# Both halves of x under one weight load, and a rearranged first stage, in a two-layer encoder on one core

## The chip, the cores and the metric

One core of one Trainium2 chip runs the whole program in one launch. The metric is device time in microseconds (us) per execution; lower is better. The profile is one further execution of the same program, recorded by the hardware profiler. TensorE is called PE, its weight loads PEld, VectorE DVE, ScalarE ACT, GpSimd POOL; SP only issues DMAs here.

## The reference

A sequence of 256 tokens of width 2048 is normalised and sent through two layers. Each layer projects it by one wide matrix, runs four attentions on the pieces, gates and sums their projections, and normalises again:

```
x = layer_norm(x, emb_ln_g, emb_ln_b)
for l in range(2):
    h = x @ w_in[l]                     # 2048 columns -> q, k, v, z of A, B, C, D and the gates
    ya, yb, yc, yd = attentions(h)      # A and D rotate part of q and k, B has a bias, C normalises q and k
    proj = (y * silu(z)) @ w_branch[l]  # for each of the four
    merged = sum(proj * sigmoid(gates + b_gate[l]))
    x = layer_norm(ALPHA * x + merged @ w_out[l], ln_g[l], ln_b[l])
```

All is float32.

## The kernel before

**Three products for one.** Matmuls run on a rounded float32 type. To keep float32 accuracy, x and each weight are split in a high part (the rounded value) and a low part (the rest). A product is then high·high + low·high + high·low. For x the parts are the tiles `th` and `tl` (each 128 x 16 x 256: 16 tiles of 128 features, 256 tokens). For a weight they are `whi`, made by a cast on ACT (line 140), and `wlo`, made by a subtraction on DVE (line 141). Weights come in groups of 512 KB (`wraw`, four buffers, loaded by SP), and each group is split into one of four buffers of `whi` and `wlo`.

**Two ways to project.** `chunk` (lines 172 to 198) puts tokens on the partitions of the result: x's tile is the stationary operand, 512 (or 384) weight columns move, three matmuls for each k and each half of the tokens (lines 182, 183, 186). `chunk_t` (lines 200 to 216) makes transposed columns for the q and k of A, B and D: 128 weight columns are the stationary operand, 256 tokens move. For each k of 16 and each of four blocks of 128 columns it issues three matmuls into the same half bank:

```
nc.tensor.matmul(o, lhsT=hi[:, kk, cs], rhs=tl[:, k, :], ...)   # line 212
nc.tensor.matmul(o, lhsT=hi[:, kk, cs], rhs=th[:, k, :], ...)   # line 213
nc.tensor.matmul(o, lhsT=lo[:, kk, cs], rhs=th[:, k, :], ...)   # line 214
```

A layer has ten such calls (A and B two each, D six), the program twenty. The accumulators are PSUM banks from the pool `psw` (four); a call of either function takes two. A and D then rotate the result (`rotate`, lines 307 to 314), and A and B split it for their score matmuls (`split_evac`, lines 218 to 225, `qkT`).

**First stage.** `first_chunk` (lines 551 to 594) overlaps the first normalisation with the first 512 columns of the projection. Half 0 of x (tokens 0 to 127) is centred on DVE (line 535), transposed on PE in four parts `c` (`x_t`, line 542), scaled on ACT (line 545), and multiplied unsplit with the raw weights (line 571, "plain" below). Half 1 goes the same way, but is split, and multiplied in the three-product form (lines 587, 588, 591, "split pass"). The split of half 0 is made for later columns. `keep_x` (lines 596 to 610) finishes x's scale and shift row-wise and stores it to DRAM; the generator is stepped through in the first stage's neighbours.

**What sets the order.** The code is traced in program order, and a scheduler then orders the instructions of each engine; pools decide what waits for a buffer. Inside `manual_schedule` (line 670) the instructions of PE, ACT and DVE keep the written order among themselves, while others may be put between them. Attention is written as generators (`attend_a` and so on) that advance one step at each weight group (`step`).

Of the kernel before, what the change touches and what calls it, by code (L numbers as in the profile page):

```python
# [88 lines left out]
def hybrid_encoder(ctx: ExitStack, tc: tile.TileContext, a: dict, out: bass.AP):  # L89
# [28 lines left out]
    th = big.tile([P, NK, SEQ], F32R, name="th")  # L118
    tl = big.tile([P, NK, SEQ], F32R, name="tl")
# [4 lines left out]


    def load_raw(src, off, n):
        raw = wrw.tile([P, KG, NCH], F32, tag="wraw", name="wraw")
        nc.sync.dma_start(
            out=raw[:, :, :n],
            in_=src[off:off + P * KG * n].rearrange("(p k n) -> p k n", p=P, k=KG),  # L130
        )
        return raw

    def split_w(raw, n, spare=None, eng=None):
        if spare is None:
            hi = whl.tile([P, KG, NCH], F32R, tag="whi", name="whi")
            lo = whl.tile([P, KG, NCH], F32R, tag="wlo", name="wlo")
        else:
            hi, lo = ((ysp if tag == "yl" else att).tile([P, KG, NCH], F32R, tag=tag, name="wsp", bufs=bufs) for tag, bufs in spare)
        nc.scalar.copy(hi[:, :, :n], raw[:, :, :n])  # L140
        (eng or nc.vector).tensor_tensor(out=lo[:, :, :n], in0=raw[:, :, :n], in1=hi[:, :, :n].bitcast(F32), op=ALU.subtract)  # L141
        return hi, lo

    def load_w(src, off, n, spare=None):
        return split_w(load_raw(src, off, n), n, spare)
# [26 lines left out]
    def chunk(src, off, n, nkt, lh, ll, perm=False, apart=False):  # L172

        acc = [psw.tile([P, NCH], F32, tag="pw", name="pw") for _ in range(2)]
# [23 lines left out]
        return [t[:, :n] for t in acc]  # L198

    def chunk_t(src, off):  # L200

        acc = [psw.tile([P, NCH], F32, tag="pw", name="pw") for _ in range(2)]
        ng = NK // KG
        for g in range(ng):
            hi, lo = load_w(src, off + g * P * KG * NCH, NCH)
            for b in range(4):
                o = acc[b // 2][:, (b % 2) * SEQ:(b % 2 + 1) * SEQ]
                cs = slice(b * P, (b + 1) * P)
                for kk in range(KG):
# [97 lines left out]
    def rotate(ps, dst, rows, cos, sin):  # L307

        xs = att.tile([P, 1024], F32, tag="rb", name="xs", bufs=1)[:rows, :NCH].rearrange("p (n j m) -> p n j m", n=2, j=2)
        for r in range(0, rows, 32):  # L310
            nc.scalar.copy(xs[r:r + 32], ps[r ^ 32:(r ^ 32) + 32])  # L311
        nc.vector.tensor_tensor(out=dst, in0=ps[:rows], in1=cos, op=ALU.mult)
        nc.vector.tensor_tensor(out=xs, in0=xs, in1=sin, op=ALU.mult)
        nc.vector.tensor_tensor(out=dst, in0=dst, in1=xs, op=ALU.add)
# [200 lines left out]
    nc.scalar.dma_start(out=gT, in_=a["emb_ln_gT"])  # L515
    nc.scalar.dma_start(out=bT, in_=a["emb_ln_bT"])

    def load_x(half):
        for c in range(4):
            nc.sync.dma_start(out=merged[:, half, c * NCH:(c + 1) * NCH], in_=a["x"][half * P:(half + 1) * P, c * NCH:(c + 1) * NCH])  # L520

    def center(half):

# [9 lines left out]
        for c in range(4):  # L533
# [17 lines left out]
    def first_chunk(src, off):  # L551
# [16 lines left out]
        for c in range(4):  # L568
# [3 lines left out]
            if c == 0:  # L572
                center(1)
# [344 lines left out]
```

## Time and profile before

| | |
|---|---|
| median of 3 runs | 2149.33 us (2148.49 to 2150.35) |
| the profiled execution's own time | 2148.79 us |
| its span, first to last instruction | 2147.0 us |
| PE busy | 2115.2 us, 99% of the span |
| DVE busy | 1292.0 us, 60% |
| ACT busy | 984.4 us, 46% |
| moved by DMA | 410.55 MB, mean 191 GB/s |
| mean granted PE clock | 0.997 |

Busy time of PE is modelled at the ends of matmuls, so it tells that PE hardly rests, not that every matmul runs at its peak. The distance from one start to the next tells what a matmul costs in a row. The clock that the throttle granted is shown as a share of full speed (2.4 GHz); 0.5 is 1.2 GHz. It is recorded from its first change on, so in the first 16 us the rows' durations have to tell it.

### The profile page before, as it was taken

Reading aid. Unit: us, or ns where it says so; the run is one execution under the profiler, and the core shown is the slowest. Engines: PE = TensorE matmul, PEld = TensorE weight load, DVE = VectorE, ACT = ScalarE, POOL = GpSimd, SP = SyncE. Lnnn points to the kernel's source line nnn. Section 1 sums busy time; section 2 is a strip of 40 time slices with the busy share of each in tenths; the row PEclk is TensorE's granted clock in tenths of the full one; section 3 lists DMA queues with packets and bytes.
Section 4 is the critical chain, followed back from the end, with each engine's and each line's share of the span. In section 5 each row is a group of like instructions: output and inputs, shape, how many; then the busy total and the mean of one; then the engine's idle time right before and its main releaser. Section 6 shows DMA issues by size and latency. Waiting matters only on the chain.

```text
span 2147.0 us, 29625 instructions
## 1 busy us (share of the span) xinstructions
PE 2115.2 (99%) x11720; PEld 1852.4 (86%) x11720; DVE 1292.0 (60%) x1555; ACT 984.4 (46%) x1279; POOL 32.7 (2%) x34
## 2 busy tenths in 40 slices
PE   6999999999999999999999999999999999999997
PEld 4899888888999988888888998888889999888886
DVE  6765655765555565556576655557655555555566
ACT  5554444444454444444445544444444454444442
POOL 0000100000000000000000000000000000000000
PEclk9999999999999999999999999999999999999999
DMA  8755566555555566666755555665555555566664
GB/s 252 232 171 167 190 200 199 186 184 192 186 166 175 166 198 204 215 196 220 229 199 173 168 168 186 199 194 183 185 202 177 176 157 186 193 203 211 198 213 150
DMA packets 129659, 410.55 MB, mean 191 GB/s; under 512 B 13872, under 2 KB 31280, under 8 KB 129008
## 3 DMA queue, kind: packets, MB, share of 16 engines
q1 hardware_dynamic: 129232, 408.64, 59.3%
q8 instruction: 92, 1.51, 0.3%
q14 instruction: 47, 0.39, 0.1%
q10 hardware_dynamic: 288, 0.02, 0.0%
HBM read 402.31 MB, written 6.29 MB: 190 GB/s over the span
## 4 chain that ended last, share of the span: by engine, by line
PE 95%; DMA 2%; DVE 2%; ACT 1%; issue 1%; SPq 0%; DVEq 0%; POOL 0%; ACTq 0%
PE pw L182 23%; PE pw L183 23%; PE pw L186 23%; PE pw L212 7%; PE pw L214 7%; PE pw L213 7%; PE pw L571 1%; PE pt L277 1%; DMA lnr<-in_emb_ln_b 1%; PE po L503 1%; PE po L431 1%; PE sc L489 1%; PE sc L363 0%; DMA lnr<-in_emb_ln_g 0%; PE pt L741 0%
## 5 line engine op out<-in xcount | busy, mean ns | idle before, releaser
L141 DVE TENSOR_TENSOR wlo<-wraw,whi 128x1024 fp32r<-128x1024 f32 (+1 forms) x720 | 864.2, 1203 | 702.6 <-ACT whi L140 702.1
L140 ACT CAST whi<-wraw 128x1024 fp32r<-128x1024 f32 (+1 forms) x720 | 742.7, 1033 | 984.8 <-PE pw L183 681.6
L182 PE MATMUL pw<-whi,tl 128*128 128x512 f32 (+1 forms) x1968 | 760.4, 386 | 0.4 <-DVE tl L222 0.4
L183 PE MATMUL pw<-whi,th 128*128 128x512 f32 (+1 forms) x1968 | 753.6, 383 | 0.0
L186 PE MATMUL pw<-wlo,th 128*128 128x512 f32 (+1 forms) x1968 | 593.4, 383 | 0.0
L182 PEld LDWEIGHTS pw<-whi,tl 128*128 128x128 f32 x1968 | 371.6, 189 | 65.3 <-DVE tl L222 0.6
L183 PEld LDWEIGHTS pw<-whi,th 128*128 128x128 f32 x1968 | 371.7, 189 | 64.7
L186 PEld LDWEIGHTS pw<-wlo,th 128*128 128x128 f32 x1968 | 368.7, 189 | 67.9
L212 PE MATMUL pw<-tl,whi 128*128 128x256 f32 x1280 | 366.9, 287 | 0.0
L214 PE MATMUL pw<-th,wlo 128*128 128x256 f32 x1280 | 362.1, 283 | 0.0
L213 PE MATMUL pw<-th,whi 128*128 128x256 f32 x1280 | 362.1, 283 | 0.0
L212 PEld LDWEIGHTS pw<-tl,whi 128*128 128x128 f32 x1280 | 245.3, 192 | 1.0
L213 PEld LDWEIGHTS pw<-th,whi 128*128 128x128 f32 x1280 | 245.4, 192 | 0.4
L214 PEld LDWEIGHTS pw<-th,wlo 128*128 128x128 f32 x1280 | 245.2, 192 | 0.0
L182 PE MATMUL pw<-whi,yl 128*128 128x512 f32 x256 | 100.7, 393 | 0.0
L183 PE MATMUL pw<-whi,yh 128*128 128x512 f32 x256 | 99.7, 390 | 0.0
L186 PE MATMUL pw<-wlo,yh 128*128 128x512 f32 x256 | 79.4, 390 | 0.0
L186 PEld LDWEIGHTS pw<-wlo,yh 128*128 128x128 f32 x256 | 48.1, 188 | 10.1
L183 PEld LDWEIGHTS pw<-whi,yh 128*128 128x128 f32 x256 | 48.1, 188 | 9.5
L182 PEld LDWEIGHTS pw<-whi,yl 128*128 128x128 f32 x256 | 48.1, 188 | 9.5
L311 ACT COPY xs<-pw 32x512 f32<-32x512 f32 x80 | 46.2, 577 | 11.3 <-PE pw L214 8.3
L759 DVE TENSOR_TENSOR gt<-pw,bg 128x512 f32<-128x512 f32 x64 | 43.9, 687 | 9.2 <-PE pw L186 9.2
(150 smaller groups left out, 1101.2 us busy)
## 6 DMA issues: line engine op xcount, KB each, us to landing
wraw<-in_w_in SPq DMA_DIRECT2D x544, 512.0 KB, 3.6
wraw<-in_w_branch SPq DMA_DIRECT2D x64, 512.0 KB, 3.4
wraw<-in_w_out SPq DMA_DIRECT2D x64, 512.0 KB, 4.2
wraw<-in_w_in SPq DMA_DIRECT2D x64, 384.0 KB, 3.5
bg<-in_b_gate SPq DMA_DIRECT2D x32, 256.0 KB, 4.3
xr<-x_dram SPq DMA_DIRECT2D x16, 256.0 KB, 4.5
merged<-in_x SPq DMA_DIRECT2D x8, 256.0 KB, 5.8
x_dram<-merged SPq DMA_DIRECT2D x8, 256.0 KB, 3.9
```

The lines of the kernel that those rows point to most:

```text
L140: nc.scalar.copy(hi[:, :, :n], raw[:, :, :n])
L141: (eng or nc.vector).tensor_tensor(out=lo[:, :, :n], in0=raw[:, :, :n], in1=hi[:, :, :n].bitcast(F32), op=ALU.subtract)
L182: nc.tensor.matmul(acc[half][:, :n], lhsT=tok(ll, k, half, perm), rhs=hi[:, kk, :n], start=k == 0, stop=False)
L183: nc.tensor.matmul(acc[half][:, :n], lhsT=tok(lh, k, half, perm), rhs=hi[:, kk, :n], start=False, stop=False)
L186: nc.tensor.matmul(acc[half][:, :n], lhsT=tok(lh, k, half, perm), rhs=lo[:, kk, :n], start=False, stop=k == nkt - 1)
L212: nc.tensor.matmul(o, lhsT=hi[:, kk, cs], rhs=tl[:, k, :], start=k == 0 and b % 2 == 0, stop=False)
L213: nc.tensor.matmul(o, lhsT=hi[:, kk, cs], rhs=th[:, k, :], start=False, stop=False)
L214: nc.tensor.matmul(o, lhsT=lo[:, kk, cs], rhs=th[:, k, :], start=False, stop=k == NK - 1 and b % 2 == 1)
L277: nc.tensor.transpose(pt[:, q * P:(q + 1) * P], src[:, q * P:(q + 1) * P], ident)
L311: nc.scalar.copy(xs[r:r + 32], ps[r ^ 32:(r ^ 32) + 32])
L431: nc.tensor.matmul(po[:, hh * P:(hh + 1) * P], lhsT=pT[:, (2 * hh + kt) * P:(2 * hh + kt + 1) * P], rhs=v[:, kt, vcol[hh]:vcol[hh] + P], s ...
L759: nc.vector.tensor_tensor(out=t, in0=ps[half], in1=bg, op=ALU.add)
```

## The change

Four things change.

- **x's parts side by side.** `th` and `tl` become the two halves of one tile `tx` (128 x 16 x 2 x 256). In `chunk_t` one matmul with 512 moving columns takes the place of lines 212 and 213: the stationary high weight meets low and high x at once and writes a full bank, low product in the left half, high product in the right. The low weight's matmul (256 columns) adds to the right half. A weight group is now four k by 256 columns instead of two k by 512, so each call makes 256 columns, in two banks, and there are forty calls.
- **A fold behind it.** The two halves of each bank have to be added: ACT copies the left half to SBUF, DVE adds the right half (`fold`). `rotate` then works on that SBUF tile in place; for D, ACT's copy of the 64 rows that aren't rotated falls away.
- **First stage.** 40 transposes of the identity matrix, whose result nothing reads, stand ahead of all else on PE. The written order is new: parts 0 and 1 of half 0 are transposed ahead of the first plain group, each later part one group ahead; half 1 is centred after the third plain group.
- **Loads.** The first x pieces are issued from SP and ACT in turn; SP is scheduled by hand too; the small weights (`small_weights`) and the rows of `keep_x` are issued behind the last weight load written so far, and `keep_x` is stepped through after A's two attentions.

```
+    tx = big.tile([P, NK, 2, SEQ], F32R, name="tx")
+    tl, th = tx[:, :, 0], tx[:, :, 1]
...
+        for g in range(NK // TG):
+            hi, lo = load_w(src, off + g * P * TG * TCH, TCH, kg=TG)
+            for b in range(2):
                 cs = slice(b * P, (b + 1) * P)
...
+                for kk in range(TG):
+                    k = g * TG + kk
+                    nc.tensor.matmul(acc[b], lhsT=hi[:, kk, cs], rhs=tx[:, k].rearrange("p h t -> p (h t)"), start=k == 0, stop=False)
+                    nc.tensor.matmul(acc[b][:, SEQ:], lhsT=lo[:, kk, cs], rhs=th[:, k, :], start=False, stop=k == NK - 1)
             step()
...
+    def fold(acc, dst, order=None):
+
+        t = vec.tile([P, 2, SEQ], F32, tag="tmp", bufs=3, name="fo")
+        for b in range(2):
+            nc.scalar.copy(t[:, b], acc[b][:, :SEQ])
+            x, y = acc[b][:, SEQ:], t[:, b]
+            if order:
+                x, y = order(x), order(y)
+            nc.vector.tensor_tensor(out=dst[:, b], in0=x, in1=y, op=ALU.add)
...
+            eng = nc.sync if c % 2 == 0 else nc.scalar
+            eng.dma_start(out=merged[:, half, c * NCH:(c + 1) * NCH], in_=a["x"][half * P:(half + 1) * P, c * NCH:(c + 1) * NCH])
...
+        idle = psa.tile([P, NCH], F32, tag="pa", name="idle")
+        for _ in range(WARM):
+            nc.tensor.transpose(idle[:, :P], ident, ident)
```

**PE, start of the program, before.** `pt` is a transposed piece of x, `xt` its scaled copy; lines 571 are the plain matmuls of half 0.

```order
L542 MATMUL pt<-ident,merged 128x128 x4
L571 MATMUL pw<-wraw,xt 128x512 x4
L542 MATMUL pt<-ident,merged 128x128 x4
L571 MATMUL pw<-wraw,xt 128x512 x4
L542 MATMUL pt<-ident,merged 128x128 x4
L571 MATMUL pw<-wraw,xt 128x512 x4
L542 MATMUL pt<-ident,merged 128x128 x8
L571 MATMUL pw<-wraw,xt 128x512 x4
L542 MATMUL pt<-ident,merged 128x128 x4
L587 MATMUL pw<-whi,tl 128x512
```

**PE, start of the program, now.** Line 617 is the warm-up, 558 the transposes, 595 the plain matmuls, 602 the split pass.

```order
L617 MATMUL idle<-ident 128x128 x40
L558 MATMUL pt<-ident,merged 128x128 x8
L595 MATMUL pw<-wraw,xt 128x512 x4
L558 MATMUL pt<-ident,merged 128x128 x4
L595 MATMUL pw<-wraw,xt 128x512 x4
L558 MATMUL pt<-ident,merged 128x128 x4
L595 MATMUL pw<-wraw,xt 128x512 x4
L558 MATMUL pt<-ident,merged 128x128 x4
L595 MATMUL pw<-wraw,xt 128x512 x4
L558 MATMUL pt<-ident,merged 128x128 x4
L602 MATMUL pw<-whi,tx 128x512
```

Each plain group now stands one group of transposes behind the one that it needs, where before it stood right behind it. Further on, the order before puts 56 matmuls of the first `chunk_t` (28 and 28) between the parts of the split pass; now all of the split pass stands ahead of the first `chunk_t`.

**ACT, first stage, now** (line 145 casts weights, 561 scales transposed x, 235 casts x's high part; `xt` with a number is half 1). The first cast stands ahead of all scaling, and two casts of the next weights, the `whi` rows, stand between the last two parts of half 1.

```order
L145 CAST whi<-wraw 128x1024
L561 ACTIVATE xt<-pt,bT,gT 128x128 x8
L145 CAST whi<-wraw 128x1024
...
L235 CAST tx<-xt_299 128x4x128
L145 CAST wsp<-wraw 128x1024 x2
L561 ACTIVATE xt_331<-pt,bT,gT 128x128 x4
L688 ACTIVATE le<-ls 128x2
L145 CAST whi<-wraw 128x1024
L235 CAST tx<-xt_331 128x4x128
L561 ACTIVATE xt_355<-pt,bT,gT 128x128 x4
L145 CAST whi<-wraw 128x1024
L235 CAST tx<-xt_355 128x4x128
```

**ACT, end of the first `chunk_t` call, now** (line 226 is the fold's copy, 325 the rotation's). Before, the rotation's four copies stood there alone, reading PSUM. The first copy now waits for PE's last matmul into the first bank, and casts are queued behind it.

```order
L145 CAST whi<-wraw 128x1024 x3
L226 COPY fo<-pw 128x256
L145 CAST whi<-wraw 128x1024
L226 COPY fo<-pw 128x256
L325 COPY xs<-xr 32x512 x4
L145 CAST whi<-wraw 128x1024 x2
L235 CAST qkT<-xr 128x512
```

## Rows read from the trace of the kernel before

**Rows 1.** The page: PE's busy time, and the chain that ended last, by engine.

```profile
PE 2115.2 (99%) x11720; PEld 1852.4 (86%) x11720; DVE 1292.0 (60%) x1555; ACT 984.4 (46%) x1279; POOL 32.7 (2%) x34
...
PE 95%; DMA 2%; DVE 2%; ACT 1%; issue 1%; SPq 0%; DVEq 0%; POOL 0%; ACTq 0%
```

**Rows 2.** Stretches: length, busy us (count) of PE, PEld, DVE, ACT, POOL; clock, DMA.

```profile
9.30:60.50 51.20, 42.91 (x168) 28.19 (x169) 36.92 (x53) 30.07 (x56) 2.67 (x4) 0.93 0.86 263
...
100.00:1080.00 980.00, 979.96 (x5441) 863.12 (x5440) 583.59 (x690) 450.14 (x573) 14.72 (x12) 1.00 0.60 191
```

**Rows 3.** Stretches of `chunk_t` alone and `chunk` alone; two starts at 384 columns.

```profile
550.36:596.42 46.06, 46.06 (x385) 46.05 (x384) 23.21 (x25) 20.99 (x25) 0.00 (x0) 1.00 0.56 178
266.64:402.75 136.11, 136.11 (x602) 112.65 (x602) 77.21 (x76) 57.90 (x62) 1.33 (x1) 1.00 0.60 196
...
596.43 0.34 PE L182 MATMUL pw<-whi,tl 128*128 128x384 f32 x1
...
596.60 0.34 PE L183 MATMUL pw<-whi,th 128*128 128x384 f32 x1
```

**Rows 4.** Timeline of PE, first stage: start, length, instructions [idle before, and what ended it].

```profile
9.30 1.12 PE L542 MATMUL pt<-ident,merged 128*128 128x128 f32 x4 [9.30 <-DVE merged L535]
10.96 6.28 PE L571 MATMUL pw<-wraw,xt 128*128 128x512 f32 x8 [0.55 <-ACT xt L545]
17.08 0.60 PE L542 MATMUL pt<-ident,merged 128*128 128x128 f32 x4
18.23 3.70 PE L571 MATMUL pw<-wraw,xt 128*128 128x512 f32 x8 [0.55 <-ACT xt L545]
...
26.46 1.04 PE L542 MATMUL pt<-ident,merged 128*128 128x128 f32 x8
29.66 5.40 PE L571 MATMUL pw<-wraw,xt 128*128 128x512 f32 x8 [2.17 <-ACT xt L545]
...
49.51 0.50 PE L587 MATMUL pw<-wsp,tl 128*128 128x512 f32 x1 [2.82 <-DVE tl L222]
...
60.07 0.61 PE L591 MATMUL pw<-wsp,th 128*128 128x512 f32 x2
```

**Rows 5.** Stretches in which the granted clock (third from the end) is low.

```profile
30.00:32.00 2.00, 2.00 (x3) 0.70 (x3) 0.43 (x2) 2.00 (x4) 1.12 (x3) 0.50 0.88 281
50.00:52.00 2.00, 2.00 (x8) 1.54 (x7) 2.00 (x3) 0.00 (x0) 0.00 (x0) 0.58 0.85 159
```

**Rows 6.** Timeline of the other engines at the start.

```profile
0.72 1.82 SPq L520 DMA_DIRECT2D merged<-in_x  x4
1.00 0.29 POOL masks.py:199 TENSOR_SCALAR_AFFINE_SELECT ident<-ident 128x128 f32<-128x128 f32 x1
...
6.85 0.69 DVE L526 BATCH_NORM_STATS2 st<-merged 128x6 f32<-128x512 f32 x1 [0.50 <-DMA merged<-in_x]
...
10.46 1.51 ACT L545 ACTIVATE xt<-pt,bT,gT 128x128 f32<-128x128 f32 x4 [3.96 <-PE pt L542]
```

**Rows 7.** Groups by shape: line, engine, operation, count | busy us, mean ns | idle before.

```profile
L141 DVE TENSOR_TENSOR wlo<-wraw,whi 128x1024 fp32r<-128x1024 f32 x656 | 803.1, 1227 | 648.0 <-ACT whi L140 648.0
L140 ACT CAST whi<-wraw 128x1024 fp32r<-128x1024 f32 x656 | 689.4, 1052 | 919.5 <-PE pw L183 668.1 <-PE pw L213 125.6 <-issue 77.3
...
L222 DVE TENSOR_TENSOR tl<-xt,th 128x512 fp32r<-128x512 f32 x8 | 5.1, 685 | 0.0
...
L221 ACT CAST th<-xt 128x512 fp32r<-128x512 f32 x8 | 4.6, 630 | 0.1
```

**Rows 8.** Groups of the shape of the fold's two operations (256 columns from PSUM).

```profile
L338 ACT ACTIVATE zt<-pw 128x256 f32<-128x256 f32 x16 | 5.7, 385 | 7.4 <-DVE v L678 7.1
...
L222 DVE TENSOR_TENSOR yl<-pt,yh 128x256 fp32r<-128x256 f32 x8 | 3.3, 419 | 0.0
```

**Rows 9.** Waits: who waited for whom, us in total, times, longest.

```profile
ACT whi L140 <- PE pw L183: 681.6, 434, 5.2
...
PE sc L363 <- ACT qkT L221: 2.7, 2, 2.1
```

More of the change, by code (lines that the diff above doesn't have):

```diff
@@ L172, in chunk @@
     def chunk(src, off, n, nkt, lh, ll, perm=False, apart=False):
-        acc = [psw.tile([P, NCH], F32, tag="pw", name="pw") for _ in range(2)]
+        acc = acc_banks()
         ng = nkt // KG
@@ L532, in center @@
         nc.gpsimd.tensor_tensor(out=rs, in0=ve, in1=mhalf[:, 0:1], op=ALU.pow)
-        for c in range(4):
-            x = merged[:, half, c * NCH:(c + 1) * NCH]
-            nc.vector.tensor_scalar(out=x, in0=x, scalar1=mv[:, 0:1], scalar2=rs, op0=ALU.subtract, op1=ALU.mult)
+        return mv, rs
+    def center(half, c, mv, rs):
+        x = merged[:, half, c * NCH:(c + 1) * NCH]
+        nc.vector.tensor_scalar(out=x, in0=x, scalar1=mv[:, 0:1], scalar2=rs, op0=ALU.subtract, op1=ALU.mult)
     def x_t(half, c, dst):
@@ L591, in first_chunk @@
                     nc.tensor.matmul(acc[1], lhsT=tok(th, k, 1, False), rhs=lo[:, kk], start=False, stop=k == NK - 1)
-            x_split(0, c, xt[:, 4 * c:4 * c + 4])
-        tasks.append(keep_x())
+        load_x(0)
+        nc.scalar.dma_start(out=gT, in_=a["emb_ln_gT"])
+        nc.scalar.dma_start(out=bT, in_=a["emb_ln_bT"])
+        load_raws(2)
+        load_x(1)
+        load_raws(2)
+        idle = psa.tile([P, NCH], F32, tag="pa", name="idle")
+        for _ in range(WARM):
+            nc.tensor.transpose(idle[:, :P], ident, ident)
+        m0 = stats_of(0)
+        for c in range(4):
+            center(0, c, *m0)
+        split(1)
+        x0_t(0)
+        x0_t(1)
+        split(1)
+        m1 = stats_of(1)
+        plain(0)
+        x0_t(2)
+        split(1)
+        plain(1)
+        x0_t(3)
+        split(1)
+        plain(2)
+        for c in range(4):
+            center(1, c, *m1)
+        split(1)
+        x1_t(0)
+        split(1)
+        plain(3)
+        x1_t(1)
+        split(1)
+        split_pass(0)
+        split(1)
+        x1_t(2)
+        split_pass(1)
+        x1_t(3)
+        split_pass(2)
+        x_split(0, 0, xt[:, 0:4])
+        x_split(0, 1, xt[:, 4:8])
+        split_pass(3)
+        x_split(0, 2, xt[:, 8:12])
+        x_split(0, 3, xt[:, 12:16])
         return acc
@@ L602, in keep_x @@
                 t = vec.tile([P, NCH], F32, tag="bc", name="lnr")
-                load_bc(t, a[nm][cs])
+                with tc.issue_after(loads[-1]):
+                    load_bc(t, a[nm][cs])
                 rows.append(t)
@@ L656, in new_branch, with cols_t @@
             return zs, (yh, yl)
-        def cols_t(nm):
-            return chunk_t(w_in, OFFSETS[nm])
+        def cols_t(nm, part):
+            return chunk_t(w_in, OFFSETS[nm] + part * D * TCH)
         def v_tile():
@@ L674, in columns_ab @@
                 if not sw:
[L675 removed]
+                    if l == 0:
+                        with tc.issue_after(loads[-1]):
+                            sw.extend(small_weights())
+                    else:
+                        sw.extend(small_weights())
                 neglam, sg, gn, bias = sw
@@ L715, in pairs @@
             def pairs(i):
-                for ps in cols_t(f"Dqk{i}"):
+                for part in range(2):
+                    ps = cols_t(f"Dqk{i}", part)
                     h, g = divmod(len(ready), 3)
```

132 lines of the change are left out of this document (61 added, 71 removed).

## The prediction

> **What bounds the kernel now.** The page comes first: PE is busy 99% of the span and makes 95% of the chain that ended last, while DVE and ACT are at 60% and 46% [rows 1]. The table of stretches says where PE rests: of the 980 us from 100 on it is busy 979.96, but of the 51.2 us from its first instruction at 9.30 to 60.5 only 42.91, and those at a mean clock of 0.93 [rows 2]. So there are two places to gain: the 9.3 us ahead of PE's first instruction with the loose 51 us behind it, and the cost of the matmuls themselves in the dense rest.
>
> For the second I looked at stretches in which a single kind of matmul runs with no gap. `chunk_t` alone: 46.06 us for 384 matmuls (the 385th counted is the tail of the one ahead), 119.95 ns from start to start. `chunk` alone, 512 columns: 136.11 us for 600 (two are tails), 226.85 ns. At 384 columns two starts lie 0.17 us apart [rows 3]. The three fall on a line: 53.4 ns for 128 columns, and 13 ns that every matmul pays, however wide it is.
>
> **The merged matmul.** For each k and block of 128 columns three matmuls of 256 become one of 512 and one of 256: 3 x 119.95 = 359.9 before, 226.85 + 119.95 = 346.8 now, so 13.05 ns less. There are 20 calls x 16 k x 4 blocks = 1280 such units: **16.7 us**. The trace does not show this pair in turn, nor a weight load hidden alternately under 512 and 256 columns; but it shows either width with a new load for each matmul at full density (385 matmuls with 384 loads, 602 with 602), which is why I take the whole of it. The bounds are 0 (the columns streamed, 768, are the same) and 16.7.
>
> The Trainium skill, "TensorE: Matmul & The Clock Gate", section "Back-to-back issue gap", gives a matmul at full clock its columns at 2.4 GHz and a fixed 2.5 ns. By that page the edit would save, as an estimate, 1280 x 2.5 = 3.2 us. Nothing in the sum uses it: the trace has 13 ns at three widths, and the measurement decides.
>
> **The fold.** It adds 80 copies on ACT and 80 additions on DVE, each of 256 columns from PSUM. The nearest rows are an activation of that shape, 385 ns, and a subtraction, 419 ns [rows 8]: 31 us on ACT, 34 us on DVE over the program. I cost it at nothing on the path. A call lasts 32 x 346.8 ns = 11.1 us, and takes two of four banks, so a fold has until the end of the next call to free its own. In those 11.1 us DVE has four subtractions of 1.23 [rows 7], two additions and three rotation passes of about 0.68 (the 512-column row of [rows 7]): 7.8 us. ACT has less. What is queued behind the fold's second copy on ACT are weight casts, and these have room: they wait 681.6 us for PE to release buffers [rows 9], so they run as far ahead as four buffers let them, about three groups of 2.8 us, less 1.05 for the cast and 1.23 for the subtraction: 6 us. A fold's copy can hold the queue from one bank's end to the next, four pairs or 1.4 us. If the cover were gone, the second bank's copy and addition would cost 0.80 us a call, 32 us in all.
>
> **First stage: what it takes now.** The last matmul of the split pass ends its slot at 60.5, and by then 56 matmuls of `chunk_t` have run in between, 56 x 0.12 = 6.7 us. So the stage alone takes PE to **53.8**. Its work at full clock is 28.2 us: 16 plain matmuls, recorded in two parts each, 0.43 a part (3.70 for eight, less the tail), 13.8; 48 matmuls of the split pass at 0.227, 10.9; 32 transposes at 0.11 (eight take 1.04, four 0.60 [rows 4]), 3.5.
>
> **First stage: what it takes then.** x's last piece of half 0 is in at 6.85, and the first transposes follow at 9.30, 2.45 later [rows 4, 6]. Issued from two queues, the four pieces leave SP in half of 1.82 us [rows 6]; I take 0.5 of the 0.9 (bounds 0 and 0.9, since their bytes still share the DMA engines): transposes from 8.8. The warm-up begins when the identity is there, at 1.3 [rows 6]. Forty transposes at full clock take 40 x 0.11 = 4.4 us, at half clock 8.8. In the rows the first plain group takes 6.28 for eight parts, the next 3.70, and the transposes at 17.08 are fast [rows 4]. Six parts at 0.86 and two at 0.43 make 6.0 and a tail, so the clock came up near 16: 5 us after the plain matmuls began, 7 after PE's first work. If transposes count as such work, it comes up here between 6.3 and 8.3, after 22 to 32 of them, and the rest is done by 8.3 to 9.2. I take 0.3 us of delay: plain matmuls from about 10 on at full speed.
>
> From there ACT paces the stage. Its list up to the cast of half 1's last part, as the order shows: eight weight casts at 1.05, 32 scalings in eight groups of 1.51 [rows 6], four casts of x at 0.63 [rows 7], two casts of the next weights: 8.4 + 12.1 + 2.5 + 2.1 = 25.1 us. It begins with the first cast at 8.2 (the weights behind x's pieces; estimate). Laid beside PE's list (a plain group 3.44, transposes 0.45), ACT waits for transposes about four times, 0.5 to 1.7 us, 5 in all. It ends at 38.4. DVE then has a subtraction of 1.23, half hidden, and x's of 0.69; the last 12 matmuls take 2.7: **42.9**. PE meanwhile rests once for half 1's centring (1 us) and once, 2 to 3 us, for part 2 behind the inserted cast and subtraction. Before, rests of 2.17 and 2.82 us [rows 4] were each followed by a stretch at 0.50 to 0.58 [rows 5], so one of two such falls stays likely; I charge 0.8, half of the 1.6 that eight matmuls lose at half clock (0.43 for 0.227). 43.7 against 53.8: **10.1 us**. The bounds: at best PE never rests after 8.8, 37.0, a gain of 16.8; at worst the two lists interleave no better than now, 0. I take the walk's value, nearer to the upper end, since the 56 foreign matmuls and `keep_x`'s work on DVE are out of the stage. `keep_x` (16 passes of 0.68 us on DVE, and its row loads on SP) moves into B's columns, where DVE has idle time for it.
>
> **Scores of A.** PE waited 2.7 us for the cast of `qkT` [rows 9], in both layers together. Now the first half of q and k is folded, rotated and split during the second call, so only one half's work lies behind the last matmul; the scores stand 42 instead of 45 matmuls later, 0.7 us less time. I take **2.4** (bounds 0 and 2.7).
>
> **The sum.** The profiled execution's own time is 2148.8, 0.5 below the median. 2148.8 - 16.7 - 10.1 - 2.4 = 2119.6, so against the median **2120**.
>
> **Rivals.**
> - *The warm-up doesn't warm.* Rows of before have no long run of transposes; the eight at 26.46 were followed by a rest and then a fall to 0.50, which leaves it open [rows 4, 5]. Then all forty run at half clock to 10.1, 1.3 behind x, of which 0.3 is in the sum, and the first plain group takes 6.28 instead of 3.70: 3.6 us more, **2124**. The Trainium skill, same page, "Part 4: PE-mode transpose", states just this: that transposes don't count as busy PE for the clock.
> - *No gain in the first stage*, since ACT's and DVE's lists are as long as before: 2120 + 10 = **2130**. For it: 25 us of ACT work in a row. Against: DVE loses `keep_x`, PE its foreign matmuls.
> - *The merged matmul saves nothing*, because the pair pays for its columns and the 13 ns come back at the switch of widths: 2120 + 16.7 = **2137**. The 2.5 ns of the Trainium skill, named above, would leave 3.2 of the 16.7.
> - *Slower: casts late behind the fold.* ACT works in order; if the fold's second copy holds the next cast until the call's end and the lead is gone, PE waits each call for copy, cast and subtraction, 0.385 + 1.05 + 1.23 = 2.7 us, x 40 = 107: **2227**. It begins to cost when ACT is held over 6 us; 0.7 us a call would undo the whole gain. The casts' waits for PE speak against it.
>
> **How the numbers follow.** Chances: forecast 0.69, cold warm-up 0.14, no gain in the first stage 0.07, no gain in the matmul 0.06, late casts 0.04. The forecast's own range is 2113 (first stage 16.8, scores 2.7) to 2127 (first stage 5, scores 0). With the cold warm-up and most of the third case the range is 2112 to 2130; it leaves out some 0.13. A measurement of this kernel tells about 0.2% (4 us) from no change: faster 0.95, same 0.02, slower 0.03.
>
> **What would show it.** Right: in `chunk_t` alone starts 227 and 120 ns apart in turn, with PE busy throughout; the granted clock at 1.00 when the first plain group begins, which then takes 3.7; the split pass done at 42 to 45 with no matmuls of `chunk_t` in it; no wait of PE for `qkT` over 0.5. Wrong: a pair over 355 ns; a first plain group near 6.3 us; waits of PE for `wlo` or for PSUM behind the folds; or a rest over 3 us in the split pass, on ACT's casts or on the small loads behind them.

## The result, and the profile after

The changed kernel takes **2127.28 us** in the median of 4 runs (2126.68 to 2127.61), against 2149.68 (2148.49 to 2150.35) for the kernel before on the same chip: a ratio of 0.9896, 95% interval 0.9879 to 0.9913. It is 22 us faster; 29 were forecast. The profiled execution took 2127.32 us, with a span of 2125.2, which is 21.8 less than before.

The page, where it answers to [rows 1]:

```profile
PE 2105.6 (99%) x10480; PEld 1787.3 (84%) x10480; DVE 1316.8 (62%) x1635; ACT 997.9 (47%) x1335; POOL 33.7 (2%) x34
...
PE 97%; DVE 1%; DMA 1%; ACT 0%; issue 0%; DVEq 0%; POOL 0%; SPq 0%
```

PE remains the bound. It runs 1280 matmuls fewer and the 40 transposes of the warm-up more (10480 instructions instead of 11720), and its share of the chain that ended last rises from 95% to 97%. The stretches, with the columns of [rows 2]:

```profile
1.34:4.90 3.56, 3.56 (x17) 3.56 (x18) 0.00 (x0) 0.00 (x0) 0.00 (x0) 1.00 0.75 207
4.90:7.64 2.74, 2.74 (x25) 2.50 (x23) 2.46 (x4) 1.28 (x1) 0.00 (x0) 1.00 1.06 389
9.51:45.00 35.49, 30.96 (x113) 19.40 (x113) 25.16 (x37) 27.01 (x53) 3.49 (x4) 0.95 0.71 242
39.00:42.40 3.40, 3.40 (x9) 2.64 (x9) 3.40 (x6) 3.40 (x7) 0.00 (x0) 0.50 0.67 220
...
537.52:582.62 45.10, 45.10 (x257) 39.08 (x255) 27.09 (x34) 22.41 (x30) 0.00 (x0) 1.00 0.58 181
100.00:1080.00 980.00, 979.56 (x4877) 835.30 (x4876) 611.93 (x752) 458.21 (x598) 14.58 (x11) 1.00 0.61 196
```

The reader is to see four things. The first two rows hold nothing on PE but the warm-up's 40 transposes: 17 of them in the first 3.56 us, 0.21 us each, then 23 (and the tails of two) in 2.74 us, about 0.11 from start to start; the clock is recorded from its first change on, so there the rate tells it: PE went to full clock at 4.9 us. (This moment scatters: in the eight other profiles with the same warm-up, e2 to e4 and e6 to e10 below, it lies between 4.15 and 7.46 us, always ahead of the first transposes of x.) The first stage ends at 45.0, with 4.5 us of rest in it and 3.4 us at a clock of 0.50. In the dense 980 us PE still never rests (979.56). And 45.10 us of `chunk_t` alone hold 128 pairs (the 257th matmul is the tail of the one ahead): 352.3 ns a pair, where 346.8 was forecast.

PE's timeline of the first stage, to set beside [rows 4] (line 595 plain, 602 to 606 split pass, 217 the merged matmul, 218 the low weight's):

```profile
1.34 6.30 PE L617 MATMUL idle<-ident 128*128 128x128 f32 x40 [1.34 <-POOL ident masks.py:199]
9.51 1.11 PE L558 MATMUL pt<-ident,merged 128*128 128x128 f32 x8 [1.87 <-DVE merged L551]
10.71 3.70 PE L595 MATMUL pw<-wraw,xt 128*128 128x512 f32 x8
...
22.97 0.66 PE L558 MATMUL pt<-ident,merged 128*128 128x128 f32 x4 [0.81 <-DVE merged L551]
...
26.00 1.95 PE L595 MATMUL pw<-wraw,xt 128*128 128x512 f32 x4 [0.66 <-DMA wraw<-in_w_in]
...
37.79 0.50 PE L602 MATMUL pw<-wsp,tx 128*128 128x512 f32 x1 [2.97 <-DVE tx L236]
...
41.20 1.05 PE L606 MATMUL pw<-wsp,tx 128*128 128x512 f32 x2
...
45.00 0.39 PE L217 MATMUL pw<-tx,whi 128*128 128x512 f32 x1
...
99.50 0.28 PE L218 MATMUL pw<-tx,wlo 128*128 128x256 f32 x1
...
109.56 0.28 PE L218 MATMUL pw<-tx,wlo 128*128 128x256 f32 x1
...
537.52 0.39 PE L217 MATMUL pw<-tx,whi 128*128 128x512 f32 x1
537.75 0.28 PE L218 MATMUL pw<-tx,wlo 128*128 128x256 f32 x1
537.87 0.40 PE L217 MATMUL pw<-tx,whi 128*128 128x512 f32 x1
...
540.70 0.40 PE L217 MATMUL pw<-tx,whi 128*128 128x512 f32 x1
```

The first plain group takes 3.70 us, as at full clock. One rest stands out, 2.97 us ahead of the split pass's third quarter; behind it two matmuls (line 606) take 1.05 us, where they take 0.62 elsewhere in the stage: the low clock. The last rows show that a pair has two rhythms. From 99.50 to 109.56 lie 29 pairs, 346.9 ns each, the forecast. From 537.52 to 540.70 lie nine, 353.3 ns each. Over the pairs of the program the distance from the 512 columns' start to the 256 columns' is 234.4 ns in the mean, and from there to the next 116.7: 351.1. (This is worked out from the starts in the trace, without the 48 pairs that stand behind a matmul of the attentions; these start later, before as now.)

Waits, answering to [rows 9], of PE between 9 and 2113 us and of ACT:

```profile
PE sc L378 <- ACT qkT L235: 0.4, 2, 0.2
...
ACT whi L145 <- PE pw L191: 686.5, 432, 5.1
ACT whi L145 <- PE pw L217: 112.3, 80, 2.7
...
ACT fo L226 <- PE pw L218: 17.2, 33, 1.3
```

Lines 191 now and 183 before are matmuls of `chunk`. Those of `chunk_t` are line 217 now and line 213 before, where the same wait was:

```profile
ACT whi L140 <- PE pw L213: 166.6, 99, 2.9
```

**Where the 21.8 us of span come from:** the split pass is done at 45.0 instead of the 53.8 that the prediction had worked out for before (8.8 us); 1280 pairs cost 351.1 instead of 359.7 ns, the mean of before by the same count (11.0 us); PE waits 0.4 instead of 2.7 for A's scores (2.3). The sum is 22.1, 0.3 more than the span shows.

### The profile page after: what moved, and what is told of

Its sections match the earlier page's. It is cut to its first block, busy times and chain, and to the rows that moved or that the text cites. A ratio compares the mean times of both kernels' runs of the same rounds, so it can differ in the third digit from the quotient of the medians.

```text
span 2125.2 us, 27271 instructions
## 1 busy us (share of the span) xinstructions
PE 2105.6 (99%) x10480; PEld 1787.3 (84%) x10480; DVE 1316.8 (62%) x1635; ACT 997.9 (47%) x1335; POOL 33.7 (2%) x34
## 3 DMA queue, kind: packets, MB, share of 16 engines
q8 instruction: 82, 1.34, 0.3%
## 4 chain that ended last, share of the span: by engine, by line
PE 97%; DVE 1%; DMA 1%; ACT 0%; issue 0%; DVEq 0%; POOL 0%; SPq 0%
PE pw L190 23%; PE pw L191 23%; PE pw L194 23%; PE pw L217 14%; PE pw L218 7%; PE pt L291 1%; PE po L446 1%; PE po L518 1%; PE sc L504 1%; DMA wraw<-in_w_in 0%; PE pw L595 0%; DVE wlo L146 0%; PE sc L378 0%; PE pt L806 0%; PE po L401 0%; PE pt L338 0%
## 5 line engine op out<-in xcount | busy, mean ns | idle before, releaser
L145 ACT CAST whi<-wraw 128x1024 fp32r<-128x1024 f32 (+1 forms) x720 | 742.7, 1033 | 930.3 <-PE pw L191 686.5
L190 PE MATMUL pw<-whi,tx 128*128 128x512 f32 (+1 forms) x1968 | 760.7, 387 | 0.4 <-DVE tx L236 0.4
L191 PE MATMUL pw<-whi,tx 128*128 128x512 f32 (+1 forms) x1968 | 753.6, 383 | 0.0
L194 PE MATMUL pw<-wlo,tx 128*128 128x512 f32 (+1 forms) x1968 | 593.3, 383 | 0.0
L217 PE MATMUL pw<-tx,whi 128*128 128x512 f32 x1280 | 457.0, 400 | 0.0
L190 PEld LDWEIGHTS pw<-whi,tx 128*128 128x128 f32 x1968 | 371.6, 189 | 65.9 <-DVE tx L236 0.6
L191 PEld LDWEIGHTS pw<-whi,tx 128*128 128x128 f32 x1968 | 371.8, 189 | 64.3
L194 PEld LDWEIGHTS pw<-wlo,tx 128*128 128x128 f32 x1968 | 368.6, 189 | 68.0
L218 PE MATMUL pw<-tx,wlo 128*128 128x256 f32 x1280 | 358.4, 280 | 0.0
L217 PEld LDWEIGHTS pw<-tx,whi 128*128 128x128 f32 x1280 | 240.4, 188 | 56.2
L218 PEld LDWEIGHTS pw<-tx,wlo 128*128 128x128 f32 x1280 | 241.7, 189 | 0.5
L194 PEld LDWEIGHTS pw<-wlo,yh 128*128 128x128 f32 x256 | 48.1, 188 | 10.1
L826 ACT ACTIVATE g<-gt 128x512 f32<-128x512 f32 x64 | 37.2, 623 | 7.7 <-DVE gt L824 7.7
L325 ACT COPY xs<-qkT 32x512 f32<-32x512 f32 x48 | 29.7, 619 | 23.5 <-DVE qkT L230 23.2
L226 ACT COPY fo<-pw 128x256 f32<-128x256 f32 x80 | 29.7, 371 | 17.4 <-PE pw L218 17.2
```

Source lines behind the costliest of these rows:

```text
L145: nc.scalar.copy(hi[:, :w], raw)
L190: nc.tensor.matmul(acc[half][:, :n], lhsT=tok(ll, k, half, perm), rhs=hi[:, kk, :n], start=k == 0, stop=False)
L191: nc.tensor.matmul(acc[half][:, :n], lhsT=tok(lh, k, half, perm), rhs=hi[:, kk, :n], start=False, stop=False)
L194: nc.tensor.matmul(acc[half][:, :n], lhsT=tok(lh, k, half, perm), rhs=lo[:, kk, :n], start=False, stop=k == nkt - 1)
L217: nc.tensor.matmul(acc[b], lhsT=hi[:, kk, cs], rhs=tx[:, k].rearrange("p h t -> p (h t)"), start=k == 0, stop=False)
L218: nc.tensor.matmul(acc[b][:, SEQ:], lhsT=lo[:, kk, cs], rhs=th[:, k, :], start=False, stop=k == NK - 1)
```

## The experiments

All times are medians of four runs (m1: one run); ratios are to the kernel before on the same chip (2149.42 to 2149.79 in the three sets). Diffs are against the changed kernel, unless the text says otherwise.

**e1_merge_only.** The kernel before, with the merged matmul, its weight groups and the fold alone. Against the changed kernel, the first stage and the loads are undone:

```
-            eng = nc.sync if c % 2 == 0 else nc.scalar
-            eng.dma_start(out=merged[:, half, c * NCH:(c + 1) * NCH], in_=...)
+            nc.sync.dma_start(out=merged[:, half, c * NCH:(c + 1) * NCH], in_=...)
...
-        idle = psa.tile([P, NCH], F32, tag="pa", name="idle")
-        for _ in range(WARM):
-            nc.tensor.transpose(idle[:, :P], ident, ident)
```

> The merged matmul and its fold alone; first stage, loads and their order as before. The changed kernel took 21.8 us less span than the one before, and its trace divides that: 8.8 in the first stage (the split pass done at 45.0 where 53.8 was worked out for before), 11.0 in the pairs of chunk_t (a mean of 351.1 ns for a pair against 359.7 for the three matmuls, 1280 times), 2.0 at the scores of A. Theory, the parts add up: this kernel is 11 to 13 us faster than before (2137 to 2139), pairs at 347 to 354 ns. Rival, the first stage's new order made the pairs' gain possible, or the fold costs time where keep_x is still in its old place: less than 9 us.

**e2_stage_only.** The other half: first stage, loads and `keep_x`'s place as changed, `chunk_t` and `rotate` as before:

```
-                    nc.tensor.matmul(acc[b], lhsT=hi[:, kk, cs], rhs=tx[:, k].rearrange("p h t -> p (h t)"), ...)
-                    nc.tensor.matmul(acc[b][:, SEQ:], lhsT=lo[:, kk, cs], rhs=th[:, k, :], ...)
+                    nc.tensor.matmul(o, lhsT=hi[:, kk, cs], rhs=tl[:, k, :], ...)
+                    nc.tensor.matmul(o, lhsT=hi[:, kk, cs], rhs=th[:, k, :], ...)
+                    nc.tensor.matmul(o, lhsT=lo[:, kk, cs], rhs=th[:, k, :], ...)
```

> The first stage, the warm-up and the loads alone; chunk_t with its three matmuls of 256 columns as before, no fold. Theory, the parts add up: 8 to 10 us faster than before (2140 to 2142), the split pass done near 45. Rival, part of the first stage's gain hangs on the merged matmul: under 6 us.

Measured: e1 **2139.02** (ratio 0.9947, 0.993 to 0.9963), 10.8 less than before; e2 **2140.69** (0.9956, 0.9941 to 0.997), 9.1 less. Together 19.9, where both at once gave 22.4. The waits of PE tell where most of the rest is. In e1, then in e2:

```profile
PE sc L378 <- ACT qkT L235: 3.0, 2, 2.8
```

```profile
PE pt L331 <- DVE ys L407: 2.4, 1, 2.4
PE sc L371 <- ACT qkT L229: 1.1, 2, 0.6
```

The merged matmul alone leaves the wait for A's scores as it was (3.0 against 2.7 in [rows 9]). It shrinks to 1.1 with the first stage alone, and to 0.4 with both. e2 has a wait of its own besides, 2.4 us of a transpose in the attention. The wait for A's scores can be told by layers: before it is 2.10 us in the first and 0.57 in the second, in e1 2.77 and 0.18, in e2 0.57 and 0.57, in the changed kernel 0.18 and 0.18. So the merged matmul's order takes it from 0.57 to 0.18 in a layer, and the new first stage takes away what the first layer has on top. In e1 the long run of pairs takes the same 45.10 us for 128 as in the changed kernel:

```profile
550.30:595.40 45.10, 45.10 (x257) 39.21 (x256) 26.96 (x33) 22.18 (x31) 0.00 (x0) 1.00 0.55 181
```

So the shortfall of the matmul term belongs to the merged matmul itself, not to the new first stage.

**e3_same_widths.** Is it the alternation of widths? In each group and bank four matmuls of 512 columns stand in a row, then four of 256:

```
                 for kk in range(TG):
                     k = g * TG + kk
                     nc.tensor.matmul(acc[b], lhsT=hi[:, kk, cs], rhs=tx[:, k]..., ...)
+                for kk in range(TG):
+                    k = g * TG + kk
                     nc.tensor.matmul(acc[b][:, SEQ:], lhsT=lo[:, kk, cs], rhs=th[:, k, :], ...)
```

> The changed kernel, but in each weight group and bank the four matmuls of 512 columns run first, then the four of 256. In the changed kernel the pair takes two rhythms, 353.3 ns in long undisturbed stretches and 346.7 in some short ones, where the widths by themselves give 226.85 + 119.95 = 346.8. Theory, the 6.5 ns belong to the alternation of widths: with one alternation for four pairs a pair takes 347 to 349 ns everywhere, and the kernel is 3 to 5 us faster than the changed one (2122 to 2124). Rival, they belong to the 512-column matmul itself, with x as its moving operand: 350 to 354, no change (within 2 us of 2127).

**e4_left_half.** Or the columns that the second matmul writes? It adds its product to the left half of the bank, which the fold adds in anyway:

```
-                    nc.tensor.matmul(acc[b][:, SEQ:], lhsT=lo[:, kk, cs], rhs=th[:, k, :], ...)
+                    nc.tensor.matmul(acc[b][:, :SEQ], lhsT=lo[:, kk, cs], rhs=th[:, k, :], ...)
```

> The changed kernel, but the low weight's matmul adds to the left half of the bank (the fold adds both halves, so the sum is the same), away from the columns that the 512-column matmul writes last. Theory, the 6.5 ns belong to the alternation of widths: the same two rhythms, within 2 us of 2127. Rival, they come of writing the same columns right behind the matmul before: a pair at 347, 5 us faster (2122).

Measured: e3 **2127.53** (0.9894, 0.988 to 0.9909), e4 **2127.84** (0.9895, 0.9881 to 0.991): neither moves the time. e4 has the same two rhythms, 353.3 and 346.7 ns, so the written half is not the cause. e3's long run of 128 pairs (the next window):

```profile
538.63:583.52 44.89, 44.89 (x257) 39.26 (x256) 27.18 (x34) 22.64 (x31) 0.00 (x0) 1.00 0.56 183
```

350.7 ns a pair: better than 352.3, but short of the 347 to 349 that alternation as the cause was to give. The mean over the program, by the count above, is 350.0, 1.1 under 351.1 and 1.4 us in all. e3's profile loses as much in the first stage: its long rest is 4.02 us, the low clock lasts 6.8 us instead of 3.4, and `chunk_t` begins at 46.3 instead of 45.0. So the unmoved time hides a small gain, and e3 alone left the cause open.

**m1_pairs_alone.** The disputed cost by itself. This kernel leaves the encoder out and runs only rows of matmuls of the same type and tiles, with nothing beside them; its own time, 254.32 us, is no time of the encoder. `wide(k)` is both parts of x for one k, `stat(t, k)` a weight piece of 128 columns, `h2` and `h4` are the high weights cut in pieces of 512 and 256 columns, `l4` the low ones.

```
for k in range(96):                      # widths apart: 512 columns, then (further down) three of 256
    nc.tensor.matmul(o, lhsT=stat(h4, k), rhs=wide(k), ...)
...
for k in range(96):                      # the changed kernel's pair
    nc.tensor.matmul(o, lhsT=stat(h4, k), rhs=wide(k), ...)
    nc.tensor.matmul(o[:, SEQ:], lhsT=stat(l4, k), rhs=th[:, k % NK], ...)
...
for k in range(96):                      # roles exchanged: x stationary, weights moving
    nc.tensor.matmul(o, lhsT=th[:, k % NK, 0:P], rhs=h2[:, k % 2], ...)
    nc.tensor.matmul(o[:, SEQ:], lhsT=th[:, k % NK, P:], rhs=h4[:, k % 4], ...)
```

> Runs of matmuls by themselves, with x and one weight group loaded and split beforehand and no other engine at work; everything else of the computation is left out, so its time is no time of the kernel. Eight runs of 96 units in a row: 512 columns with x stationary and a weight moving; 512 with a weight stationary and x moving; the same with one piece of x moving each time; 512 with x stationary and x moving; the pair of the changed kernel; the pair with the 256 columns from another tile; a pair of 512 and 256 with x stationary and weights moving; three of 256. Theory A, x as moving operand under changing weights makes 512 columns slow: the first run 227 ns, the second 233, the seventh (pair with roles exchanged) 347. Theory B, alternating widths makes it: second run 227, fifth to seventh 351 to 354. Theory C, neighbours on other engines or DMA make it: all runs at 227 or 347.

Measured, in stretches of 96 matmuls of 512 columns (weights stationary, x moving), 96 pairs as in the changed kernel, 96 pairs with the roles exchanged, and 288 matmuls of 256 columns; what the counts have over these is tails:

```profile
45.38:67.14 21.76, 21.76 (x98) 18.02 (x96) 0.69 (x1) 0.00 (x0) 0.00 (x0) 1.00 0.00 0
110.66:144.57 33.91, 33.91 (x193) 29.43 (x192) 0.00 (x0) 0.00 (x0) 0.00 (x0) 1.00 0.00 0
178.49:212.41 33.92, 33.92 (x194) 29.42 (x193) 0.00 (x0) 0.00 (x0) 0.00 (x0) 1.00 0.00 0
212.41:246.97 34.56, 34.56 (x290) 34.51 (x288) 0.00 (x0) 0.00 (x0) 0.00 (x0) 1.00 0.00 1
```

21.76 / 96 = 226.7 ns and 34.56 / 288 = 120.0: apart, a pair's two matmuls cost 346.7, as forecast from [rows 3]. In turn they cost 33.91 / 96 = 353.2, with no DMA and no other engine at work, and the same with the roles of the operands exchanged. Three rows that are not shown agree: 512 columns with one piece of x, and with x in both places, 21.76 us each; the pair with the 256 columns from another tile, 33.92. The first row, x stationary and a weight moving, begins at the low clock (427 ns from start to start) and settles at 227 as well. A pair also turns its destination, from a whole bank to half of it; but the rows of before change bank or half bank every six matmuls and cost 226.85 and 119.95 [rows 3], no more than these rows that never change it (226.7 and 120.0). So it is the turn of widths that costs 6.5 ns a pair, and it needs nothing of the kernel around it.

**e5_no_warm.** The 40 transposes ahead of all else are taken out:

```
-        idle = psa.tile([P, NCH], F32, tag="pa", name="idle")
-        for _ in range(WARM):
-            nc.tensor.transpose(idle[:, :P], ident, ident)
```

> The changed kernel without the 40 warm-up transposes. In the changed kernel the granted clock rose at 4.9 us, while nothing but these transposes had run. Theory, they buy the full clock for the first plain groups: the first group takes 6.3 us instead of 3.70 and the kernel is 2 to 4 us slower than the changed one (2129 to 2131). Rival, later rests of PE take the loss up, or the clock would have risen by then anyway: within 1 us of 2127.

Measured: **2128.74** (2127.77 to 2132.67; 0.9909, 0.9894 to 0.9924), 1.5 us over the changed kernel, less than the theory's 2 to 4. The two ranges of four runs miss each other by 0.2 us, so the size is uncertain. Its profile is that of the longest run. PE's timeline there:

```profile
9.24 1.97 PE L558 MATMUL pt<-ident,merged 128*128 128x128 f32 x8 [9.24 <-DVE merged L551]
11.01 5.80 PE L595 MATMUL pw<-wraw,xt 128*128 128x512 f32 x8
```

The first transposes take 1.97 instead of 1.11 us and the first plain group 5.80 instead of 3.70: cold, 3.0 us dearer. The clock rose at 15.4 here. In the median half of that comes back; that ACT paces what follows, as the prediction had it, would explain it, but was not tried apart. In the profiled run nothing comes back: `chunk_t` begins at 48.4, 3.4 us late, with a low clock of 6.8 us ahead of it instead of 3.4.

**e6_sp_only.** x's pieces all from SP's queue again:

```
-            eng = nc.sync if c % 2 == 0 else nc.scalar
+            eng = nc.sync
```

> The changed kernel with all x pieces issued from SP, in the same order. The changed kernel's first transposes of x started at 9.51, and before's at 9.30, where 8.8 was forecast. Theory, two queues bring x no earlier, as the DMA engines are full by then: first transposes between 9.3 and 9.9, the kernel within 1 us of 2127. Rival, they do help and something else is late: first transposes after 10, 0.5 to 1.5 us slower.

Measured: **2127.2** (2126.08 to 2127.68; 0.9897, 0.9881 to 0.9914): no change in the time. The first x transposes come at 10.01, which is where the rival had them:

```profile
10.01 1.12 PE L558 MATMUL pt<-ident,merged 128*128 128x128 f32 x8 [1.76 <-DVE merged L551]
```

With one queue they come at 9.30 (before, [rows 4]), 9.86 (e1) and 10.01, in the mean 9.7; with two at 8.73 to 9.51 in nine profiles (the changed kernel, e2 to e5 and e7 to e10), in the mean 9.2. That points to the half microsecond that was forecast, but single profiles scatter as much. The equal times don't settle it: in e6's profile the clock doesn't fall behind the long rest (2.95 us), which alone saves it 1.7 us against the changed kernel's, and `chunk_t` begins only 0.9 earlier, at 44.07.

**e7_casts_behind.** The rest of 2.97 us. ACT and DVE around it, in the changed kernel:

```profile
34.83 1.04 ACT L145 CAST whi<-wraw 128x1024 fp32r<-128x1024 f32 x1 [0.85 <-DMA wraw<-in_w_in]
35.78 0.61 ACT L235 CAST tx<-xt 128x512 fp32r<-128x512 f32 x1
```

```profile
35.91 1.22 DVE L146 TENSOR_TENSOR wlo<-wraw,whi 128x1024 fp32r<-128x1024 f32 x1 [1.68 <-ACT whi L145]
37.05 0.68 DVE L236 TENSOR_TENSOR tx<-xt,tx 128x512 fp32r<-128x512 f32 x1
```

ACT stops for 0.85 us on a weight load, then casts weights that only the first `chunk_t` needs; DVE's subtraction for them, 1.22 us, stands ahead of the one that PE waits for. In e7 these casts are queued behind half 1's last cast:

```
+            casts.append(nc.scalar.copy(hi, src).ins)        # in split_evac
...
-                    ps = cols_t(f"{br}qk{u}", b)
+                    if first and l == 0:
+                        with tc.issue_after(casts[3]):
+                            ps = cols_t(f"{br}qk{u}", b)
+                    else:
+                        ps = cols_t(f"{br}qk{u}", b)
```

> The changed kernel, but on ACT the weight casts of the first chunk_t call are queued behind the cast of half 1's last part. In the changed kernel PE rested 2.97 us ahead of the third quarter of the split pass, since DVE's subtraction for part 2 stood behind such a cast and its subtraction, and the clock fell to 0.50 behind the rest. Theory, these casts make the rest: it shrinks under 1 us, the clock stays up, chunk_t starts at 41 to 42 instead of 45.0, and the kernel is 3 to 4 us faster (2123 to 2124). Rival, the casts are only late elsewhere: chunk_t waits for its first weights, and less than 1 us is left.

Measured: **2122.92** (2122.54 to 2123.23; 0.9878, 0.9864 to 0.9893), 4.4 us under the changed kernel. PE's timeline:

```profile
34.81 0.50 PE L603 MATMUL pw<-wsp,tx 128*128 128x512 f32 x1 [0.49 <-DVE tx L237]
...
40.38 0.61 PE L218 MATMUL pw<-tx,whi 128*128 128x512 f32 x2
41.17 0.38 PE L219 MATMUL pw<-tx,wlo 128*128 128x256 f32 x1 [0.17 <-DVE wlo L147]
```

The rest is 0.49 instead of 2.97, the clock doesn't fall behind it, and `chunk_t` begins at 40.4 instead of 45.0. What was moved comes late by 0.17 us there.

**e8_eights and e9_sixteens.** e7 with longer rows of one width: in e8 all eight matmuls of 512 columns of a weight group, then its eight of 256; in e9 two weight groups at a time, sixteen and sixteen:

```
+        for g in range(0, NK // TG, 2):
+            ws = [load_w(src, off + (g + i) * P * TG * TCH, TCH, kg=TG) for i in range(2)]
+            pairs = [(b, i, kk, (g + i) * TG + kk) for b in range(2) for i in range(2) for kk in range(TG)]
+            for b, i, kk, k in pairs:
+                nc.tensor.matmul(acc[b], lhsT=ws[i][0][:, kk, b * P:(b + 1) * P], rhs=tx[:, k]..., ...)
+            for b, i, kk, k in pairs:
+                nc.tensor.matmul(acc[b][:, SEQ:], lhsT=ws[i][1][:, kk, b * P:(b + 1) * P], rhs=th[:, k, :], ...)
+            step(2)
```

> The kernel with the casts queued behind (2122.9), and in chunk_t all eight matmuls of 512 columns of a weight group, then its eight of 256. The runs of matmuls alone showed 226.67 and 120.0 for either width kept up, and 354.2 for a pair in turn whatever the operands; four and four made 350.5. Theory, a turn of widths costs some 15 ns each way round, once settled: 348 to 349 a pair with eight and eight, 2 to 4 us faster than 2122.9 (2119 to 2121). Rival, the low parts come late where they are needed in a row, or a pair stays near 350.5: within 1 us of 2122.9.

> As the kernel with eights, but two weight groups at a time: sixteen of 512, then sixteen of 256. Theory, turns of widths: 347.5 a pair, another 1 us (2118 to 2120). Rival, two of the four buffer pairs now come free together, so casts come late and PE waits at groups: slower than with eights.

Measured: e8 **2121.69** (2121.1 to 2123.56; 0.987, 0.9853 to 0.9886), 1.2 us less than e7, which its range doesn't tell from it. In its profile the attentions have a wait of 1.1 us, which takes back part of what the pairs gain. e9 **2118.41** (2118.24 to 2119.67; 0.9854, 0.9839 to 0.9869), 4.5 us under e7 and the fastest version here: 8.9 us under the changed kernel, 31.3 under the kernel before. Their long runs of 128 pairs, e8 and then e9:

```profile
534.07:578.74 44.67, 44.67 (x258) 39.33 (x257) 27.16 (x33) 22.42 (x30) 0.00 (x0) 1.00 0.57 185
```

```profile
533.44:577.95 44.51, 44.51 (x258) 39.36 (x257) 26.18 (x34) 22.62 (x31) 0.00 (x0) 1.00 0.56 184
```

(The expectation's 354.2 for a pair in turn is 353.2 over the whole row of m1.) A pair costs 352.3, 350.7, 349.0 and 347.7 ns with one, four, eight and sixteen matmuls of a width in a row: the fewer turns, the nearer to 346.7. The means over the program, by the count above, are 351.1, 350.0, 349.0 and 347.8; from the first to the last it is 4.2 us for 1280 pairs, and e9 gained 4.5 over e7. Over 346.7, a round from one width to the other and back costs 6.5 ns in m1's pairs, but 4 x 4.0, 8 x 2.3 and 16 x 1.0, or 16 to 18 ns, with four and more in a row. That is why four in a row gained so little.

**e10_fold_twice.** The fold's price. Its copy and its addition are done twice, with the same values:

```
             nc.scalar.copy(t[:, b], acc[b][:, :SEQ])
...
+            nc.vector.tensor_tensor(out=dst[:, b], in0=x, in1=y, op=ALU.add)
+            nc.scalar.copy(t[:, b], acc[b][:, :SEQ])
             nc.vector.tensor_tensor(out=dst[:, b], in0=x, in1=y, op=ALU.add)
```

> The changed kernel with the fold's copy and addition done twice (the same values again): 80 more copies on ACT, 30 us, and 80 more additions on DVE, 34 us. Theory, the fold lies wholly beside PE's matmuls: within 1.5 us of 2127, but up to 1 us at the scores of A, whose inputs come 0.8 us later. Rival, ACT or DVE has no room in chunk_t: each call loses up to 0.8 us, 10 to 32 us in all.

Measured: **2129.32** (2128.93 to 2129.67; 0.9903, 0.9889 to 0.9918), 2.0 us over the changed kernel for some 63 us of added work (80 copies of 0.371 and 80 additions of 0.418), a little more than the 1.5 expected. PE's new waits:

```profile
PE pt L340 <- DVE ys L416: 1.3, 1, 1.3
PE pt L340 <- DVE ys L452: 0.9, 1, 0.9
```

They stand in the attentions, 2.2 us together, where DVE is late, and not at the scores of A (0.3). By the profiles the price is higher than by the medians: e10's clock doesn't fall in the first stage, `chunk_t` begins at 43.45 instead of 45.00, and what follows takes 3.8 us longer: 2.5 of waits, and 1.2 of longer distances behind the attentions' transposes. In `chunk_t` itself PE waits for no fold even when it is doubled: from start to start its matmuls take 454.5 us in all in both kernels.

## Why the prediction was right, and where it was off

The time is inside the range, 7 us above the forecast. The mechanisms of the merged matmul, the fold and the first stage are there, that of A's scores in part; one term accounts for most of the miss.

- **The merged matmul, forecast 16.7, measured 11.0: the mis-sized term.** The step said that the trace "does not show this pair in turn", and took the price of each width from stretches of one width. m1 shows that both prices hold, 226.7 and 120.0, and that their sum doesn't: 353.2 in turn. That is the mechanism of the rival in which "the 13 ns come back at the switch of widths", at half its size: 6.5 ns in a long undisturbed row, 4.3 in the kernel's mean. e4 excludes which half is written, m1 the operands and the neighbours, and e9 gets most of it back with fewer turns. The bounds of 0 and 16.7 held it.
- **2.5 or 13 ns a matmul.** By m1, 512 columns take 226.7 ns; the columns at 2.4 GHz are 213.3 of it, which leaves 13.4, and 256 columns leave 13.3. The Trainium skill, "TensorE: Matmul & The Clock Gate", "Back-to-back issue gap", has 2.5 there, in a formula that this section gives for an isolated matmul (the prediction left that condition out); by it the edit would have been worth, as an estimate, 3.2 us. The measured 11.0 decides for the rows.
- **The first stage, forecast 10.1, measured 8.8.** Its end was forecast at 43.7 and came at 45.0. The rests are those that the walk had: 0.81 for half 1's centring (1 forecast) and 2.97 behind the inserted cast and subtraction (2 to 3), to which a load added 0.66. That ACT paces the stage held until the long rest: its list began at 8.18 (8.2 forecast), and the cast of half 1's last part ended at 39.3 (38.4). Two sizes were off. x came at 9.51 instead of 8.8, so that plain matmuls began at 10.71 instead of "about 10". And the clock did fall behind the long rest, which costs 1.7 (3.4 us at half speed) and was charged at 0.8. The walk's last sum is half a microsecond too long as it stands (38.4, half of 1.23, 0.69 and 2.7 make 42.4, not 42.9), so the nearness of the end is in part luck.
- **The cold warm-up: refuted.** 17 transposes in the first 3.56 us and 23 in the next 2.74 show the clock rising under transposes alone, at 4.9 us, where 6.3 to 8.3 was estimated; over nine profiles it rose at 4.15 to 7.46, in four of them inside the estimate. The Trainium skill, same page, "Part 4: PE-mode transpose", holds that transposes don't count as busy PE for the clock; for these float32 transposes the trace says otherwise. Without them (e5) the first groups are 3.0 us dearer, near the rival's 3.6, but only some 1.5 of it reaches the end in the median.
- **No gain in the first stage: refuted** by 45.0 against 53.8, and by e2, 9.1 us faster with that part alone.
- **Scores of A, forecast 2.4, measured 2.3: right in part by luck.** The explanation given, one half's work behind the last matmul instead of two, is worth 0.39 us a layer (0.57 to 0.18, e2 against the changed kernel), 0.8 in all. The other 1.5 is what the first layer waited beyond the second's 0.57. It goes with the new first stage and loads (e2), and stays without them (e1 still waits 3.0). What in these takes it away was not taken apart.
- **The fold at nothing on the path: held.** ACT's copies wait 17.2 us for PE in 33 places, 1.3 at the longest (1.4 forecast); PE never waits for `wlo`, so late casts, the slower rival, did not come. But the row that the step rested on was not that of `chunk_t`: the 681.6 of [rows 9] are waits for `chunk`'s matmuls, and now 686.5. The waits for `chunk_t`'s fell from 166.6 to 112.3, so a third of the casts' slack there is used up, by the fold or by the shorter calls, which was not told apart. e10 doubles the fold and loses 2.0 us, none of it in `chunk_t`.

**What stays open.** Why a turn of widths costs, and what puts a row of pairs into one rhythm or the other (346.9 ns from 99.50 on, 353.3 from 537.52 on, in the same kernel). And when the clock falls behind a rest: it did after 2.97 us in the changed kernel and 3.28 in e4, and did not after 2.95 in e6 and 3.32 in e10; before, it did after 2.17 [rows 4, 5].

## What to carry to other kernels

A price read from a row of equal instructions holds for a row of equal instructions: where a change mixes shapes, the mix has a price of its own, to be bounded, or measured by itself in a kernel of nothing else. When two kinds of matmul can be ordered freely, runs of one width, as long as the buffers allow, beat turns. In a start-up phase, look at what stands ahead of the awaited instruction on the engines that feed PE: moving casts that nobody awaited yet was worth 4.4 us here, against some 1.5 for the warm-up and, for the second load queue, nothing that the times show. And where a rest and a fall of the clock can hide a gain of the same size, compare profiles stage by stage, not only medians (e3, e6, e10).

## What the runs showed of the hardware

- A float32 (rounded type) matmul of 512 columns behind one of 256, and so on in turn, each with a new stationary operand, costs 353.2 ns a pair, where the two in rows of their own cost 346.7. With 4, 8 and 16 in a row it is 350.7, 349.0 and 347.7: a round of turns costs 6.5 ns when each matmul turns, and 16 to 18 when four or more stand in a row.
- Pairs in turn have two rhythms, each of which holds for many pairs: 346.9 ns (29 pairs from 99.50) and 353.3 (nine from 537.52).
- Transposes of a float32 identity bring the granted clock up from 1.2 to 2.4 GHz by themselves: 0.21 us each up to 4.9 us, 0.11 from there. In nine profiles with the same 40 transposes from 1.34 on, the rise came at 4.15 to 7.46 us, behind 13 to 28 of them.
- Rests of PE of about 3 us (2.95 to 3.32) were followed by a stretch at the low clock in some profiles and not in others, at the same place of nearly the same program. Before, one of 2.17 was followed by such a stretch too.
